# Seven block products for the output of a SwiGLU feed-forward, with weight sums made in DRAM

## The chip, the cores and the metric

The kernel runs on one core of a Trainium2 chip. The metric is the device time of one execution, in microseconds (us). A core has a matrix engine (TensorE, PE in the profile; PEld is its loading of stationary operands), a vector engine (VectorE, DVE), a scalar engine (ScalarE, ACT), a general engine (GpSimd, POOL) and a queue engine (SyncE, SP), which here only issues transfers. POOL issues transfers too, among them all that add to what is in the destination.

## The reference

One decoder layer on 512 tokens of width 1024, in float32: half a SwiGLU feed-forward, a mixer (a state-space scan beside differential attention), cross-attention into 256 memory positions, half of a second SwiGLU feed-forward, and a final norm. The change is in the last but one step:

```
def swiglu(h, w_in, w_out):
    gate, up = jnp.split(h @ w_in, 2, axis=-1)
    return (jax.nn.silu(gate) * up) @ w_out

x = x + 0.5 * swiglu(rms_norm(x, norm_ffn2_w), ffn2_w_in, ffn2_w_out)   # 1024 -> 2 x 2816 -> 1024
return rms_norm(x, norm_final_w)
```

## The kernel before

Activations lie transposed, features on the 128 partitions and the 512 tokens along the row; x is eight such tiles. A float32 matrix product is made of three matmuls in a shorter format. Each operand is split in a high part (ACT copies it to fp32r) and a low part (VectorE subtracts that from the original), and the product is high x high + high x low + low x high. split_into (line 146) issues the two instructions. Weights come from DRAM on SP into six buffers wr of 128x1024, and are split into three buffers wh and wl, so that the split of a weight block waits for the matmuls that used the block three before.

A feed-forward goes through its 22 tiles of hidden features in three parts of 8, 8 and 6 (THIRDS). In each part, quads make the hidden tiles, and then an output product adds them to x.

- quad (line 235) makes two tiles of gate and two of up by a scheme of seven block products in place of eight (Winograd's form of Strassen's). Weights are in four blocks b11, b12, b21, b22, and the products need the sums t = b12 + b11, then t + b22 and again + b21 (lines 252 and 254, on VectorE), and m7 = b12 + b22. The first and the last of these are made while loading: raw_w (line 221) loads one block on SP and adds the other with a transfer that POOL issues. The activations' sums, by halves of the tokens (H = 256), are made once for a feed-forward, in block_sums (line 190).
- ffn_quads (line 380) gates: two products with the norm's row, tanh on ACT, three operations on VectorE, and the split of two hidden tiles g.
- The output product of the first feed-forward, and of the first two parts of the second, is by feature: for each of eight output tiles proj (line 272) adds nf x 3 matmuls of 512 columns, and lines 448 and 449 add it to x. This is eight products where the quads have seven.
- The last part of the second feed-forward is by token (class Close, line 1033), so that the result comes out in rows of tokens. For four blocks of 128 tokens and two halves of the width it adds nf x 3 matmuls, with g as the stationary operand; x is transposed on TensorE (turned); then come the update, the final norm (squares on ACT, a power on POOL) and the writing, block by block.

The order of the work is written by generators in Order (line 51). Dense generators run one after the other, a chain is spawned with a delay in estimated TensorE time and steps in when its time has come. SP's queue keeps the order in which the program is traced; the other engines' queues are ordered by a planner from that order, by what it reckons to be ready. Every engine works through its queue in order and waits at the first instruction that isn't ready. The mixer runs between the feed-forwards. In it POOL issues the loads of the attention bias (line 623) and of r (line 763), computes inverse roots (lines 311 and 697) and some sums; upd_2 (line 1018) ends the cross-attention and prepares the second feed-forward. The layout of the weights in DRAM is made on the host, in layout (line 1114).

Of the kernel before, what the change touches and what calls it, by code (L numbers as in the profile page):

```python
# [17 lines left out]
P = 128  # L18
# [12 lines left out]
NSLOT = 56  # L31
NHALF = 14
# [6 lines left out]
MASKED = 8e30  # L39
LAMBDA_INIT = 0.8 - 0.6 * math.exp(-0.3 * 0)  # L40
# [54 lines left out]
def body(tc, a, dbg=None):  # L95
# [22 lines left out]
    def s4(s):  # L118
        return sp.tile([P, 2, 2, T // 2], F32, tag=s, name=nm(s), bufs=1)
# [66 lines left out]

    def hl(pair, sl):
        return pair[0][:, sl], pair[1][:, sl]

    def block_sums(k0, gain, raw):  # L190
# [4 lines left out]
        s12, s34 = s2("s12"), s2("s34")  # L195
        V.tensor_tensor(s12[:, :H], fe[:, H:], fo[:, H:], ALU.subtract)
        V.tensor_tensor(s34[:, :H], fe[:, :H], fe[:, H:], ALU.subtract)
        V.tensor_tensor(s12[:, H:], s12[:, :H], fe[:, :H], ALU.subtract)
        V.tensor_tensor(s34[:, H:], s12[:, H:], fo[:, :H], ALU.add)
        s12, s34 = split("s12", s12), split("s34", s34)  # L200
        lo, hi = slice(0, H), slice(H, T)
        return {
            "11": hl(raw[k0], lo), "12": hl(raw[k0 + 1], lo), "22": hl(raw[k0 + 1], hi),
            S1: hl(s12, lo), S2: hl(s12, hi), S3: hl(s34, lo), S4: hl(s34, hi),
        }
# [29 lines left out]
    def quad(xs, src):  # L235
# [7 lines left out]
        m1, t, m3, m2, m7 = raw_w(b11), raw_w(b12, b11), raw_w(b22), raw_w(b21), raw_w(b12, b22)  # L243
# [8 lines left out]
        V.tensor_tensor(t, t, m3, ALU.add)  # L252
        yield from add_product(b_ps, split_w(t), xs, S2, False)
        V.tensor_tensor(t, t, m2, ALU.add)
# [3 lines left out]
        yield from add_product(a_ps, split_w(m2), xs, "12", False)  # L258
# [4 lines left out]
        yield from add_product(b_ps, split_w(t), xs, "22", False)  # L263
# [113 lines left out]
    def halves(t):  # L377
        return t.rearrange("p (f t) -> p f t", f=2)

    def ffn_quads(xs, wq, st, nq, g, ahead=None):  # L380
        for q_ in range(nq):
            made = None
            for made in quad(xs, next(wq)):
                if made is None:
                    yield
            gs, us = made
            if q_ == nq - 1 and ahead is not None:
                ahead()
            gate, th = s4("gate"), s4("th")
            for i in range(2):  # L390
                row = st.row[:, None, i * H : (i + 1) * H].to_broadcast([P, 2, H])
                V.tensor_tensor(gate[:, i], halves(gs[i]), row, ALU.mult)
            S.activation(th, gate, AF.Tanh, scale=0.5)
            V.scalar_tensor_tensor(gate, th, 1.0, gate, ALU.add, ALU.mult)
            for i in range(2):
                V.tensor_tensor(th[:, :, i], halves(us[i]), gate[:, i], ALU.mult)
            for f in range(2):
                g.append(split("g", th[:, f].rearrange("p a b -> p (a b)")))
            yield
# [11 lines left out]
    def ffn(h, xs, st, wq, wo, on_final=None, first=None, plain=None, close=None, at_out=None):  # L411
        row4 = None
        wq = iter(wq)
        for ti, (f0, nf) in enumerate(THIRDS):
            g = []
            at_end = ti == len(THIRDS) - 1
            if at_end and close is not None:
                close.begin()
            nq = nf // 2
            if ti == 0 and first is not None:  # L420
                for made in ffn_first(h, first):
                    if made is None:
                        yield
                    else:
                        g.append(split("g", gated(*made, st.row)))
                for n in range(NPLAIN - 2):
# [3 lines left out]
                    g.append(split("g", gated(pg, pu, st.row)))  # L430
                    for k0 in range(2 * n, 2 * n + 2, 2):
                        xs.append(block_sums(k0, C_FFN1, h))
# [752 lines left out]
```

## Time and profile before

| | |
|---|---|
| time, median of 3 runs | 1340.49 us (1339.56 to 1343.92) |
| time of the profiled execution | 1342.28 us |
| its span, first to last instruction | 1340.4 us |
| TensorE, VectorE, ACT, POOL busy | 99%, 71%, 47%, 8% of the span |
| granted TensorE clock | 0.997 |
| second feed-forward, first quad to last matmul | some 1000 to 1333 us |
| transfers | 167.89 MB, mean 125 GB/s |

A row of a group has the line, engine and operation, what it writes and reads with shapes, how often, the busy time with the mean ns of one, and the idle time before it with what ended it. A matmul's own duration is longer than its distance to the next, since they overlap; the distance is read from the chain of waits, whose rows are the start, the length, the engine, the tile, the line and the count. Rows of a queue have the start, the length and, in brackets, the idle time before and what ended it. "Landing" is the time from a transfer's issue to its last byte.

### The profile page before, as it was taken

To read this page: it belongs to the slowest core of one execution; us is meant where nothing else is said; L and a number is where in the kernel's file an instruction comes from. 1 tells how busy PE (TensorE), PEld (TensorE's weight loads), DVE (VectorE), ACT (ScalarE), POOL (GpSimd) and SP (SyncE) were. 2 spreads that over 40 slices of the span, in tenths; PEclk is the share of its full clock that TensorE was granted. 3 is DMA by queue.
4 is the path that set the end of the run, shared out by engine and by line. 5 is a ranking of instruction groups with operands and counts; after the bars stand their busy time and mean duration, and the time that the engine had idled before them with its cause. 6 is when DMAs were issued, how large, how long until landed. Compare 5 with 4: busy or idle time off the path is not lost.

```text
span 1340.4 us, 19873 instructions
## 1 busy us (share of the span) xinstructions
PE 1321.4 (99%) x7831; PEld 1149.7 (86%) x7831; DVE 951.1 (71%) x1480; ACT 631.5 (47%) x1070; POOL 104.0 (8%) x123
## 2 busy tenths in 40 slices
PE   8999999999999999999999999999999999999997
PEld 7888999899897778877888887888889989998996
DVE  6775688477886586557877777556788747875774
ACT  6442455144554465346654656334455424542453
POOL 1000001010020001100011031000011000000000
PEclk9999999999999999999999999999999999999999
DMA  7434577466352214421173574321347645745641
GB/s 269 110 111 127 127 205 236 114 139 192 126 168 64 87 36 91 146 91 56 48 140 78 96 140 152 105 70 64 89 117 178 180 129 124 195 139 126 174 111 63
DMA packets 52156, 167.89 MB, mean 125 GB/s; under 512 B 6632, under 2 KB 9168, under 8 KB 52064
## 3 DMA queue, kind: packets, MB, share of 16 engines
q1 hardware_dynamic: 43056, 136.67, 32.1%
q0 software_dynamic: 9008, 29.97, 13.7%
q8 instruction: 61, 1.00, 0.3%
q14 instruction: 31, 0.25, 0.1%
HBM read 164.45 MB, written 4.77 MB: 126 GB/s over the span
## 4 chain that ended last, share of the span: by engine, by line
PE 91%; DVE 3%; DMA 1%; ACT 1%; issue 1%; POOL 1%; POOLq 0%; ACTq 0%; DVEq 0%
PE po L140 17%; PE qb L218 12%; PE qe L218 8%; PE pm L140 8%; PE qa L218 8%; PE pxbc L140 7%; PE pk L140 3%; PE pq L140 3%; PE pcq L140 3%; PE pv L140 3%; PE pz L140 3%; PE pf L140 2%; PE pg L140 2%; PE pu L140 2%; PE ps L140 2%; DMA r<-cum_d 1%
## 5 line engine op out<-in xcount | busy, mean ns | idle before, releaser
L149 ACT ACTIVATE wh<-wr 128x1024 fp32r<-128x1024 f32 (+2 forms) x285 | 292.5, 1028 | 386.1 <-PE po L140 117.4
L150 DVE TENSOR_TENSOR wl<-wr,wh 128x1024 fp32r<-128x1024 f32 (+2 forms) x285 | 337.8, 1186 | 105.6 <-ACT wh L149 103.3
L140 PE MATMUL po<-gh,wh 128*128 128x512 f32 x304 | 118.6, 392 | 0.0
L140 PE MATMUL po<-gl,wh 128*128 128x512 f32 x304 | 118.1, 390 | 0.0
L140 PE MATMUL po<-gh,wl 128*128 128x512 f32 x304 | 117.9, 389 | 0.0
L218 PE MATMUL qa<-hmh,wl 128*128 128x256 f32 x304 | 86.2, 284 | 0.0
L218 PE MATMUL qa<-hml,wh 128*128 128x256 f32 x304 | 86.0, 283 | 0.0
L218 PE MATMUL qa<-hmh,wh 128*128 128x256 f32 x304 | 86.0, 283 | 0.0
L448 DVE TENSOR_TENSOR upd<-po,row 128x512 f32<-128x512 f32 x40 | 27.6, 691 | 74.2 <-PE po L140 74.0
L140 PEld LDWEIGHTS po<-gh,wh 128*128 128x128 f32 x304 | 56.9, 188 | 13.6 <-ACT gh L149 2.1
L140 PEld LDWEIGHTS po<-gl,wh 128*128 128x128 f32 x304 | 57.1, 188 | 12.6 <-DVE gl L150 1.0
L140 PEld LDWEIGHTS po<-gh,wl 128*128 128x128 f32 x304 | 57.1, 188 | 11.6
L218 PEld LDWEIGHTS qa<-hmh,wl 128*128 128x128 f32 x304 | 58.3, 192 | 0.4 <-DVE wl L150 0.4
L218 PEld LDWEIGHTS qa<-hmh,wh 128*128 128x128 f32 x304 | 58.3, 192 | 0.2
L218 PEld LDWEIGHTS qa<-hml,wh 128*128 128x128 f32 x304 | 58.3, 192 | 0.2
L140 PE MATMUL pxbc<-hnh,wh 128*128 128x512 f32 x128 | 52.3, 408 | 0.0
L140 PE MATMUL pxbc<-hnl,wh 128*128 128x512 f32 x128 | 50.2, 392 | 0.0
L140 PE MATMUL pxbc<-hnh,wl 128*128 128x512 f32 x128 | 50.2, 392 | 0.0
L639 ACT ACTIVATE ec<-ec,mn 128x512 f32<-128x512 f32 (+3 forms) x64 | 35.4, 555 | 25.0 <-DVE mn L638 25.0
L226 POOL DMA_DIRECT2D wr<-in_f2q x22 | 19.0, 863 | 362.0 <-DVE wl L150 114.2
L218 PE MATMUL qe<-s12h,wh 128*128 128x256 f32 x152 | 44.0, 290 | 2.7 <-ACT wh L149 1.7
L218 PE MATMUL qe<-s12h,wl 128*128 128x256 f32 x152 | 43.8, 288 | 0.8 <-DVE wl L150 0.8
(375 smaller groups left out, 3779.8 us busy)
## 6 DMA issues: line engine op xcount, KB each, us to landing
wr<-in_f2q SPq DMA_DIRECT2D x55, 512.0 KB, 4.0
wr<-in_f1q SPq DMA_DIRECT2D x40, 512.0 KB, 4.3
wr<-in_f2q POOLq DMA_DIRECT2D x22, 512.0 KB, 6.9
wr<-in_f2o SPq DMA_DIRECT2D x22, 512.0 KB, 4.2
wr<-in_f1q POOLq DMA_DIRECT2D x16, 512.0 KB, 6.4
wr<-in_f1o SPq DMA_DIRECT2D x16, 512.0 KB, 4.7
wr<-in_wxbc SPq DMA_DIRECT2D x16, 512.0 KB, 3.5
wr<-in_f1i SPq DMA_DIRECT2D x8, 512.0 KB, 6.9
```

Source lines behind the costliest of these rows:

```text
L140: nc.tensor.matmul(out, w, x, start=start, stop=stop)
L149: S.activation(hi, src, AF.Copy),
L150: V.tensor_tensor(lo, src, hi.bitcast(F32), ALU.subtract),
L218: nc.tensor.matmul(out, a_[:, wc], b_, start=first and f == 0 and kp == 0 and j == 0, stop=kp == n - 1 and j == 2, skip_group_check=True)
L226: last_sum[:] = [G.dma_start(raw, m, accum_op=ALU.add).ins]
L448: V.tensor_tensor(upd, po, row4, ALU.mult)
L639: S.activation(ec[:, :n], ec[:, :n], AF.Exp, bias=mn, scale=-1.0, accum_out=sm[c][:, i : i + 1])
```

## The change

The output product of the second feed-forward is now by token in all three parts, and made by the same scheme of seven products as the quads. The blocks are: hidden tiles in pairs (even, odd), tokens in halves of 256, the width in halves of 512. g is the stationary operand, in blocks of 128 tokens, and the weights stream in 512 columns. Each product keeps its sums for two blocks of tokens in two PSUM banks.

What comes with it:

- The hidden tiles are kept as blocks and as sums of blocks (block_tiles, sums_of), made right after gating, on ACT and VectorE, once for each quad.
- Four sums of the output weights' blocks are made in DRAM (out_sums): for each part and sum, one copy from DRAM to DRAM on SP, and two transfers that add on POOL. The chain is spawned 60 us (estimated) after the end of the first feed-forward.
- In the quads of the second feed-forward (by_transfer), t + b22 is no longer made on VectorE. b22 is loaded a second time into a buffer t2, and a transfer on POOL adds t to it. The next sum, t4, is made on VectorE after m2 has been split, in m2's buffer.
- x is transposed right after the cross-attention (turn, 22 us after its last update), in place.
- Updates and the final norm are by block of tokens; in the last part the last product takes its blocks one after the other (by_pair).
- The slots for 128x512 tiles go from 56 to 55, those for 128x256 from 14 to 16. ffn is now ffn1 for the first feed-forward, whose work is the same, and ffn2. The host lays the weights out in blocks.

The diff, cut to its core:

```diff
-NSLOT = 56
-NHALF = 14
+NSLOT = 55
+NHALF = 16
+    def sums_of(b11, b21, b22, b12, pair=None):
+        s31, s24 = s2("s31"), s2("s24")
+        if pair is None:
+            V.tensor_tensor(s31[:, :H], b11, b21, ALU.subtract)
+            V.tensor_tensor(s31[:, H:], b21, b22, ALU.subtract)
+        else:
+            V.tensor_tensor(halves(s31), *pair, ALU.subtract)
+        V.tensor_tensor(s24[:, :H], s31[:, H:], b11, ALU.subtract)
+        V.tensor_tensor(s24[:, H:], s24[:, :H], b12, ALU.add)
+        s31, s24 = split("s31", s31), split("s24", s24)
+        lo, hi = slice(0, H), slice(H, T)
+        return {S3: hl(s31, lo), S1: hl(s31, hi), S2: hl(s24, lo), S4: hl(s24, hi)}
...
-        m1, t, m3, m2, m7 = raw_w(b11), raw_w(b12, b11), raw_w(b22), raw_w(b21), raw_w(b12, b22)
+        m1, t = raw_w(b11), raw_w(b12, b11)
+        if by_transfer:
+            t2, m2, m7, m3 = raw_w(b22, t), raw_w(b21), raw_w(b12, b22), raw_w(b22)
+            t4 = m2
...
-        V.tensor_tensor(t, t, m3, ALU.add)
-        yield from add_product(b_ps, split_w(t), xs, S2, False)
-        V.tensor_tensor(t, t, m2, ALU.add)
+        if not by_transfer:
+            V.tensor_tensor(t2, t, m3, ALU.add)
+        yield from add_product(b_ps, split_w(t2), xs, S2, False)
...
+        w2 = split_w(m2)
+        if by_transfer:
+            V.tensor_tensor(t4, t2, m2, ALU.add)
+        yield from add_product(a_ps, w2, xs, "12", False)
...
+    def block_tiles(g):
+        def made(th):
+            raw = split("g", th[:, 2:4].rearrange("p a b -> p (a b)"))
+            b11 = [s2("g11" + p_, R32, (P, H)) for p_ in "hl"]
+            split_into(*b11, th[:, 0])
+            lo, hi = slice(0, H), slice(H, T)
+            g.append({"11": tuple(b11), "22": hl(raw, lo), "12": hl(raw, hi)} | sums_of(*(th[:, i] for i in range(4)), pair=(th[:, 0:2], th[:, 1:3])))
+        return made
...
+            od.spawn(out_sums(), 60.0)
...
+    def out_sums():
+        for t, (to, of) in enumerate(((B12, B11), (B12, B22), (B22, 0), (B21, 2))):
+            for c in range(len(THIRDS)):
+                blocks = a[f"f2b{c}"]
+                nc.sync.dma_start(wsum[c][t], blocks[to])
+                yield 5.0
+                more = wsum[c][of] if t > 1 else blocks[of]
+                for k in range(0, more.shape[1], D):
+                    ks = slice(k, min(k + D, more.shape[1]))
+                    G.dma_start(wsum[c][t][:, ks], more[:, ks], accum_op=ALU.add)
+                    yield 3.0
+
+    def out_blocks(c, g, col4, last):
+        blocks = a[f"f2b{c}"]
+        n = len(g)
+        parts = [(k, min(k + 2, n)) for k in range(0, n, 2)]
...
+        def some(ps, w, which, part, t, first):
+            ts = slice(t * P, (t + 1) * P)
+            for k in range(*part):
+                (wh, wl), (gh, gl) = w, g[k][which]
+                ws = slice((k - part[0]) * T, (k - part[0] + 1) * T)
+                for j, (a_, b_) in enumerate(((gh, wh), (gl, wh), (gh, wl))):
+                    nc.tensor.matmul(ps, a_[:, ts], b_[:, ws], start=first and k == 0 and j == 0, stop=k == n - 1 and j == 2, skip_group_check=True)
+                yield
...
+        both = [product(a_ps, blocks[B11], "11", True), product(e_ps, sums[0], S1, True)]
+        for _ in parts:
+            for m in both:
+                for _ in range(2 * 2):
+                    if next(m, 1) is None:
+                        yield
...
+        for t in range(2):
+            S.activation(b_ps[t], a_ps[t], AF.Copy)
...
+        yield from product(b_ps, sums[2], S2)
+        for t in range(2):
+            u2.append(s2("u2"))
+            S.activation(u2[t], b_ps[t], AF.Copy)
+            V.tensor_tensor(e_ps[t], e_ps[t], u2[t], ALU.subtract)
+        yield from product(a_ps, blocks[B21], "12")
+        for t in range(2):
+            update(t, 0, a_ps[t])
+        yield from product(b_ps, sums[1], S3)
+        for t in range(2):
+            c22 = s2("c22")
+            V.tensor_tensor(c22, p5[t], b_ps[t], ALU.subtract)
+            update(t + 2, 1, c22)
+        yield from product(e_ps, blocks[B22], S4)
+        for t in range(2):
+            update(t, 1, e_ps[t])
+            if last is not None:
+                last(t)
+        for t, m in enumerate([product(b_ps, sums[3], "22", by_pair=last is not None)]):
+            yield from m
+        for t in range(2):
+            update(t + 2, 0, b_ps[t])
+            if last is not None:
+                last(t + 2)
```

More of the change, by code (lines that the diff above doesn't have):

```diff
@@ L375, in gated, with ffn_quads @@
         return gate
[L377 to L384, printed above, removed]
+    def ffn_quads(xs, wq, st, nq, made, places, by_transfer=False):
+        for _ in range(nq):
+            for out in quad(xs, next(wq), by_transfer):
+                if out is None:
                     yield
-            gs, us = made
-            if q_ == nq - 1 and ahead is not None:
-                ahead()
+            gs, us = out
             gate, th = s4("gate"), s4("th")
@@ L1098, in body @@
+    od.add(ffn2())
     od.run()
```

236 lines of the change are left out of this document (128 added, 108 removed).

## The prediction

> **What bounds the kernel now.** I read the page first, then the busy time by stretches, then the chain of waits, then the groups by shape, and last the queues of VectorE and of the transfers inside one quad.
>
> ```profile
> span 1340.4 us, 19873 instructions
> PE 1321.4 (99%) x7831; PEld 1149.7 (86%) x7831; DVE 951.1 (71%) x1480; ACT 631.5 (47%) x1070; POOL 104.0 (8%) x123
> ```
>
> TensorE is busy 99% of the span. What it no longer has to do is gained, as long as the other queues deliver in time. The stretches of the second feed-forward show how much room those have; the columns are the stretch, its length, then PE, PEld, DVE, ACT, POOL, clock, DMA share and GB/s. The second row is one quad (seven products over 256 columns), the third one output product; the first lies in the mixer.
>
> ```profile
> 425.00:560.00 135.00, 135.00 (x706) 108.63 (x705) 90.16 (x192) 72.16 (x172) 10.87 (x13) 1.00 0.33 89
> 1027.16:1047.32 20.16, 20.16 (x171) 20.16 (x170) 16.85 (x19) 10.75 (x13) 1.70 (x2) 1.00 0.75 182
> 1067.48:1111.41 43.93, 43.92 (x195) 35.89 (x194) 24.50 (x29) 10.66 (x12) 2.56 (x3) 1.00 0.49 129
> ```
>
> TensorE has no gap in any of them, at full clock. In a quad VectorE is busy 16.85 of 20.16 us; in the output product 24.50 of 43.93. The chain of waits gives the price of a matmul:
>
> ```profile
> 1053.09 2.88 PE qb L218 x24
> 1058.84 2.88 PE qb L218 x24
> 1064.60 2.88 PE qb L218 x24
> 1067.48 5.47 PE po L140 x24
> 1072.96 38.45 PE po L140 x168
> 1301.89 1.64 PE pxf L144 x15
> ```
>
> A matmul of 512 columns costs 38.45 / 168 = 0.2289 us, one of 256 columns 2.88 / 24 = 0.12 us, a transpose 0.11 us. The output product starts on the heels of the last quad (1064.60 + 2.88 = 1067.48), so even the gating of the last quad is covered now.
>
> **The change on TensorE.** The groups by shape give the counts of the two old output stages, by feature (po) and by token (pf), one of three equal rows of each, then the transposes and their copies:
>
> ```profile
> L140 PE MATMUL po<-gh,wh 128*128 128x512 f32 x128 | 49.8, 391 | 0.0
> L140 PE MATMUL pf<-wfh,gh 128*128 128x512 f32 x48 | 18.9, 401 | 0.0
> L144 PE MATMUL pxf<-ident,x 128*128 128x128 f32 x32 | 4.5, 272 | 0.0
> L1050 ACT ACTIVATE xt<-pxf 128x512 f32<-128x512 f32 x8 | 4.5, 592 | 6.3 <-PE pxf L144 6.3
> ```
>
> That is 3 x (128 + 48) = 528 matmuls of 512 columns. The new stage has seven products, each of (4, 4, 3) tile pairs x 2 token blocks x 3 parts: 168 + 168 + 126 = 462, and one matmul with ones. 65 fewer x 0.2289 = **-14.9 us**. The 32 transposes stay; they move from the end into the first quads (turn), with eight ACT copies of 0.59 us, where ACT is busy 10.75 of 20.16: nothing gained or lost.
>
> **The change on VectorE and ACT.** Prices:
>
> ```profile
> L150 DVE TENSOR_TENSOR wl<-wr,wh 128x1024 fp32r<-128x1024 f32 x98 | 119.8, 1223 | 31.8 <-ACT wh L149 31.3
> L150 DVE TENSOR_TENSOR gl<-th,gh 128x512 fp32r<-128x512 f32 x22 | 14.9, 687 | 2.3 <-ACT gh L149 2.3
> L196 DVE TENSOR_TENSOR s<-fe,fo 128x256 f32<-128x256 f32 x4 | 1.7, 424 | 0.1
> L1082 DVE SCALAR_TENSOR_TENSOR xt<-pf,col,xt 128x512 f32<-128x512 f32 x8 | 6.0, 750 | 7.1 <-PE pf L140 7.1
> L149 ACT ACTIVATE wh<-wr 128x1024 fp32r<-128x1024 f32 x98 | 103.7, 1059 | 152.1 <-PE po L140 60.8 <-PE qb L218 22.9 <-DVE wr L252 21.1
> L251 ACT ACTIVATE p<-qe 128x512 f32<-128x512 f32 x11 | 6.4, 579 | 0.0
> ```
>
> In an output stage of four pairs, 14 weight splits cost VectorE 14 x 1.22 = 17.1 us; eight updates of 0.75, two c22 and two subtractions of 0.69 make 8.8. That is 25.9 of 168 x 0.2289 = 38.5 us. ACT has 14 x 1.06 + 6 x 0.58 = 18.3. Each split (1.06 + 1.22) feeds 12 matmuls, 2.75 us, and three buffers look two parts ahead: covered, 0. Without that cover each part would wait up to 2.3 us.
>
> The quads are the tighter place. One of the two adds of weight blocks (t + m3, 1.22) goes to a transfer; two gl (1.37) become a raw gl 0.69, a g11 0.42, s31 0.69, two s24 of 0.42, and two lows of 0.69: 4.02. VectorE rises by 4.02 - 1.37 - 1.22 = 1.4 to about 18.3 of 20.16 us. The load is not even; this is its crowded stretch, the gating of the quad before among the splits of the next:
>
> ```profile
> 1046.71 1.23 DVE L252 TENSOR_TENSOR wr<-wr,wr 128x1024 f32<-128x1024 f32 x1
> 1053.76 1.22 DVE L150 TENSOR_TENSOR wl<-wr,wh 128x1024 fp32r<-128x1024 f32 x1
> 1055.56 1.23 DVE L150 TENSOR_TENSOR wl<-wr,wh 128x1024 fp32r<-128x1024 f32 x1
> ```
>
> The fifth product (m7) starts at 1058.84 and its low half is there at 1056.8: a margin of 2.1 us. The t4 add moves behind m2's split but stays ahead of m7's low half, and the add that leaves stood ahead of the stretch. So up to 4.02 - 1.37 = 2.65 us more may come before it: 0.5 us late, some 1.0 if the lows wait for ACT too. From below it is 0, if the queue takes the weights first. I take 0.4, nearer the margin's 0.5, for the 8 quads that have a gated quad before them: **+3.2** (0 to 8).
>
> **The transfers in a quad.** Before: five loads and two accumulating transfers (b11 onto t, b22 onto m7). After: six loads and three; the new one adds t onto t2 and needs t's own to have landed. The two queues' shares are of a stretch of 290 us (1000 to 1290); then the issues, with the median time to landing, the extremes of POOL's, what SP waits for, and one POOL issue:
>
> ```profile
> q1 hardware_dynamic: 9535, 34.73, 38.2%
> q0 software_dynamic: 2736, 9.96, 20.8%
> wr<-in_f2q SPq DMA_DIRECT2D x46, 512.0 KB, 4.2
> wr<-in_f2q POOLq DMA_DIRECT2D x19, 512.0 KB, 7.4
> ...
> DMA to landing us min/median/max: 5.3/7.4/8.0
> ...
> SPq L224 <- DVE wl L150: 196.5, 46, 13.0
> ...
> 1044.23 0.85 POOL L226 DMA_DIRECT2D wr<-in_f2q  x1 [13.34 <-DMA wr<-in_f2o]
> ```
>
> A load takes 0.382 x 290 / 34.73 x 0.524 = 1.67 us of all 16 engines, an accumulating one 0.208 x 290 / 9.96 x 0.524 = 3.17. A quad goes from 5 x 1.67 + 2 x 3.17 = 14.7 us (0.73 of it, as the stretch shows) to 19.5, 0.97. The six buffers now hold exactly one quad, and SP waits for one to be split free. t2's load can start about when m7 is split, 9.5 us after the quad's start; it lands 4.2 later, POOL issues (0.85), the addition lands 7.4 later: 21.95. Split (1.06 + 1.22): 24.2. Product t2 of the next quad starts at 20.16 + 2 x 2.88 = 25.9. Margin 1.7 us, so 0 from below. From above, landings that grow as the share does (x 0.97 / 0.73) take 3.8 us more: 2.1 late. I take 0.3, since the margin holds at today's landings, for 10 quads: **+3.0** (0 to 21). POOL stands still for t's landing; behind it waits only m7's transfer, which has two products more to land.
> The Trainium skill, page "DMA: Bandwidth & Descriptors", section "Bandwidth", puts the limit at about 358 GB/s of HBM for a core; eight of the nine transfers read HBM, an estimated 208 GB/s by that, so this term would be 0 and the sum 3.0 lower. The stretch's DMA share of 0.75 at 182 GB/s speaks against so much room.
>
> **Edges of the stages.** The gating of a third's last quad reaches its splits here:
>
> ```profile
> 1072.27 1.15 ACT L149 ACTIVATE gh<-th 128x512 fp32r<-128x512 f32 x2 [2.86 <-DVE th L396]
> ```
>
> That is 4.8 us after the quad's end at 1067.48. Its new "11" block is split second, about 1.7 us on (two ACT halves of about 0.5, a low of 0.69): 6.5 us after the quad. The interleaved first parts of two products cover 24 matmuls, 5.5 us, and one more pair 0.7 in the thirds of four: 0.3 + 0.3 + 1.0 = **+1.6** (0 to 4).
>
> **The tail.** Now the last of four token blocks ends like this:
>
> ```profile
> 1332.76 0.75 DVE L1082 SCALAR_TENSOR_TENSOR xt<-pf,col,xt 128x512 f32<-128x512 f32 x1
> 1335.33 0.54 POOL L1091 TENSOR_TENSOR frr<-fv,mhalf 128x1 f32<-128x1 f32 x1 [3.06 <-DVE fv L1089]
> 1337.07 0.38 SPq L1095 DMA_DIRECT2D out<-xt  x1
> ```
>
> The blocks are a matmul chain (18 x 0.2289 = 4.1 us) apart. After the change two blocks end together, 4.1 us before TensorE does, and the last two 2.06 us apart. The last update may queue behind another block's final multiplication, which waits for POOL: **+1.0** (0, if they interleave; 6, if four chains of 3.7 run one after the other).
>
> **The mixer.** It gets 12 copies in DRAM on SP and 24 accumulating transfers on POOL, each behind its copy: 24 x 0.85 = 20.4 us of POOL where it is busy 10.87 of 135, and where the DMA share is 0.33. Queued behind a waiting POOL are rr, ncol, bias and the r loads:
>
> ```profile
> r<-cum_d POOLq DMA_DIRECT2D x4, 256.0 KB, 12.0
> ...
> 514.56 3.04 POOL L763 DMA_DIRECT2D r<-cum_d  x4
> ...
> 530.36 0.61 ACT L821 ACTIVATE e<-r 64x512 f32<-64x512 f32 x1
> ...
> 539.80 1.02 PE py L140 x16
> ```
>
> The first r lands at 514.56 + 0.75 + 12 = 527.3 and is used at 530.4, 3 us later: the cover. A transfer in front (7.4) would exceed it by 4. I take **+0.5** (0 to 4). One slot fewer (55) and the altered block sums do the same work: 0. The sums themselves are needed after 1067: ready long before.
>
> **Sum.** -14.9 + 3.2 + 3.0 + 1.6 + 1.0 + 0.5 = **-5.6 us**. The profiled execution's own time, 1342.28, becomes 1336.7. It stands 1.8 above the median 1340.49, so the median becomes **1334.9**.
>
> **Rivals.**
> (B) All cover holds; only the tail and a little at the edges is paid: -14.9 + 1.4 = -13.5, 1327. For: TensorE shows no gap in a quad with VectorE at 84%. Against: 18.3 of 20.16 and a margin of 2.1.
> (C) VectorE and transfers together eat the gain: 1.0 in each of 11 quads, 1.6 + 1.0 at edges and tail: -14.9 + 13.6 = -1.3, 1339. For: both late arrivals fall into the same stretch of the quad. Against: they overlap rather than add.
> (D) Slower: the transfer onto t2 becomes the bound. The quad then lasts as long as buffer, load, two landings, split and m7's split. From landings of 4.2 + 7.4 = 11.6 it stalls above 13.3, and from about 14.5 the gain is gone ((14.9 - 3.1) / 10 = 1.2 a quad). At the upper end, 2.1 x 10 + 3.1 - 14.9 = +9, 1349.5. For: 0.97 of the engines. Against: the longest of POOL's landings in the old quads is 8.0.
> The Trainium skill, same page, section "Issuing engines are not separate DMA queues", says that transfers from POOL and SP interleave on the same 16 engines; by that rule D's price holds in full. The trace agrees: the two queues' prices add up to 0.73 of a quad, and the quad's row shows 0.75.
> (E) The mixer decides: POOL, waiting for copies, holds up the r loads of a group and one set of rr and ncol by 4 us each beyond their cover: 8 in place of 0.5, +1.9 in all, 1342.4. For: POOL takes its queue in order. Against: the DMA share of 0.33 there. That the products save no matmuls can't be, since the loops fix their number.
>
> **Chances.** Forecast (-2 to -11, 1329.5 to 1338.5) 0.45; B 0.22; C 0.15; D 0.14; E 0.04. A measurement of this kernel can tell about 0.3%, 4 us. Faster by more: 0.38 of the forecast and all of B, 0.60. Within: 0.07 of the forecast, 0.12 of C, 0.02 of E, 0.21. Slower: D and the rest, 0.19. The range takes in B and the nearer part of D: 1326 to 1346.
>
> **What would show it.** Right: output stages of 38.5, 38.5 and 28.8 us without gaps; waits of TensorE in the quads for wl (VectorE's term) or for wh behind a transfer (t2's term), adding up to 6 us; quads of 20.4 to 21 us. B: quads still 20.16. D: POOL's transfers landing after 9 us and quads over 21.4. E: gaps between 425 and 700 that were not there. I am wrong if the output stages themselves show gaps.

## The result, and the profile after

The changed kernel takes 1382.4 us (median of five runs, 1377.3 to 1384.4), the kernel before 1339.6 (five runs, 1338.4 to 1343.9): a ratio of 1.031, 95% interval 1.028 to 1.034. It is slower, by far more than rival D allowed; 1334.9 was forecast. The profiled execution took 1377.29 us.

The head of the profile page of the changed kernel, its span and its busy times:

```profile
span 1375.3 us, 20006 instructions
PE 1319.3 (96%) x7766; PEld 1145.8 (83%) x7766; DVE 978.0 (71%) x1533; ACT 667.3 (49%) x1124; POOL 135.0 (10%) x158
```

TensorE's 65 matmuls are gone (7831 to 7766), and yet its busy time falls by only 2 us, mostly because part of its work ran on a slower clock; and it stood still for 37 us more. The times from the first matmul of a stage to the first of the next add up to the span, so they say where the 34.9 us between the two profiled executions came from. The medians differ by 42.8, and the profiled execution of the changed kernel was its fastest of five, so some of the loss of the others isn't in this table (to about 0.1 us):

| us | before | after | difference |
|---|---|---|---|
| up to the first quad of the second feed-forward | 983.3 | 989.1 | +5.8 |
| quads, first third (with the moved transposes) | 84.0 | 89.2 | +5.2 |
| output stage, first third | 43.9 | 38.3 | -5.6 |
| quads, second third | 80.7 | 89.2 | +8.5 |
| output stage, second third | 43.9 | 38.4 | -5.5 |
| quads, last third, up to the last stage's first matmul | 60.5 | 76.1 | +15.6 |
| last stage and tail | 44.1 | 55.0 | +10.9 |

Busy times by stretch of the changed kernel (stretch, length, PE, PEld, DVE, ACT, POOL, clock, DMA share, GB/s): first output stage, second third's quads, second output stage, and then the end piece by piece.

```profile
1078.25:1116.60 38.35, 38.35 (x170) 31.38 (x169) 30.32 (x36) 20.85 (x25) 2.57 (x3) 1.00 0.71 205
1116.60:1205.75 89.15, 83.23 (x673) 82.34 (x673) 65.99 (x79) 44.00 (x55) 7.75 (x9) 0.98 0.78 207
1205.75:1244.20 38.45, 38.45 (x170) 31.42 (x169) 30.36 (x36) 20.86 (x25) 2.58 (x3) 1.00 0.68 206
1311.04:1320.35 9.31, 0.28 (x4) 0.08 (x2) 7.03 (x12) 4.36 (x7) 0.00 (x0) 0.75 0.00 0
1320.35:1325.00 4.65, 4.61 (x10) 3.21 (x11) 2.94 (x3) 1.41 (x2) 0.00 (x0) 0.50 0.43 129
1347.52:1359.93 12.41, 0.39 (x3) 0.01 (x1) 4.42 (x12) 4.50 (x10) 1.50 (x2) 0.73 0.45 148
```

The first two output stages do what the sum said: 38.35 and 38.45 us without a gap. The second third's quads have 6 us of idle TensorE in 89, and the last stage has two holes, 9.31 us ahead of it and 12.41 in it. Behind the first, ten matmuls take 4.65 us in place of 10 x 0.2289 = 2.3, at a clock of 0.50.

What TensorE waited for, over the whole execution (total, times, longest):

```profile
PE ob L1115 <- ACT wh L151: 12.0, 1, 12.0
PE oa L1115 <- ACT wh L151: 9.0, 1, 9.0
PE qb L231 <- ACT u L277: 8.4, 8, 2.6
PE py L142 <- DVE r L852: 5.1, 2, 3.8
PE qb L231 <- ACT qb L267: 3.5, 4, 1.7
```

Four places, then. In the quads the wait is for the copies u and qb out of PSUM, not for wl or for a transfer's wh, where I had looked. The chain of waits through the hole in the last stage:

```profile
1352.72 0.73 ACT x L1194
1353.46 0.33 SPq L1195
...
1353.89 0.39 SPq L1197
...
1354.34 4.37 DMA wr<-wsum
...
1358.82 1.06 ACT wh L151
...
1359.93 1.22 PE ob L1115 x2
```

SP takes its queue in order. The writes of the finished token blocks (L1195, L1197) wait for the norm's last multiplication (L1194), and the loads for the last product stand behind them. ACT at the start of the last stage:

```profile
1312.14 1.06 ACT L412 ACTIVATE th<-gate 128x1024 f32<-128x1024 f32 x1 [8.83 <-DVE gate L411]
1318.72 0.63 ACT L151 ACTIVATE s24h<-s 128x512 fp32r<-128x512 f32 x1 [0.29 <-DVE s L204]
1319.26 1.99 ACT L151 ACTIVATE wh<-wr 128x1024 fp32r<-128x1024 f32 x2
```

The splits of the first output weights come last, behind the whole gating of the last quad, though ACT had been idle for 8.83 us before it. In the mixer, POOL:

```profile
523.18 1.72 POOL L1089 DMA_DIRECT2D wsum<-wsum  x2 [7.53 <-DMA wsum<-in_f2b]
524.30 2.94 POOL L790 DMA_DIRECT2D r<-cum_d  x3
```

POOL stood 7.5 us at a sum whose copy hadn't landed, and the r loads behind it were issued 10 us later than before (514.56). In the quads, ACT:

```profile
1184.97 1.06 ACT L151 ACTIVATE wh<-wr 128x1024 fp32r<-128x1024 f32 x1 [4.01 <-DMA wr<-wr]
1185.93 1.04 ACT L412 ACTIVATE th<-gate 128x1024 f32<-128x1024 f32 x1
1187.83 0.58 ACT L267 ACTIVATE qb<-qa 128x512 f32<-128x512 f32 x1
1195.40 0.63 ACT L151 ACTIVATE s24h<-s 128x512 fp32r<-128x512 f32 x1 [1.36 <-DVE s L204]
1196.41 0.59 ACT L277 ACTIVATE u<-qb 128x512 f32<-128x512 f32 x1
```

The split of t2 waits 4 us for the new transfer, with tanh and the copy qb behind it; the sums' halves, waiting for VectorE, stand ahead of u.

### The profile page after: what moved, and what is told of

Same layout as the page of the kernel before. It is cut to its first block, busy times and chain, and to the rows that moved or that the text cites. A ratio compares the mean times of both kernels' runs of the same rounds, so it can differ in the third digit from the quotient of the medians.

```text
span 1375.3 us, 20006 instructions
## 1 busy us (share of the span) xinstructions
PE 1319.3 (96%) x7766; PEld 1145.8 (83%) x7766; DVE 978.0 (71%) x1533; ACT 667.3 (49%) x1124; POOL 135.0 (10%) x158
## 5 line engine op out<-in xcount | busy, mean ns | idle before, releaser
L142 PE MATMUL po<-gh,wh 128*128 128x512 f32 x176 | 68.8, 392 | 0.0
L142 PE MATMUL po<-gl,wh 128*128 128x512 f32 x176 | 68.5, 390 | 0.0
L142 PE MATMUL po<-gh,wl 128*128 128x512 f32 x176 | 68.4, 389 | 0.0
L231 PE MATMUL qb<-s31h,wh 128*128 128x256 f32 x152 | 44.4, 292 | 8.4 <-ACT u L277 8.4
L231 PE MATMUL qb<-s24h,wh 128*128 128x256 f32 x152 | 44.4, 292 | 3.6 <-ACT qb L267 3.5
L231 PE MATMUL qe<-s31h,wh 128*128 128x256 f32 x152 | 44.0, 290 | 1.7 <-ACT wh L151 1.7
L231 PE MATMUL qe<-s31h,wl 128*128 128x256 f32 x152 | 43.8, 288 | 0.8 <-DVE wl L152 0.8
L231 PE MATMUL qe<-s31l,wh 128*128 128x256 f32 x152 | 43.9, 288 | 0.2 <-DVE s31l L152 0.2
L231 PE MATMUL qb<-s24l,wh 128*128 128x256 f32 x152 | 43.7, 288 | 0.0
L231 PE MATMUL qb<-s24h,wl 128*128 128x256 f32 x152 | 43.7, 287 | 0.0
L474 DVE TENSOR_TENSOR upd<-po,row 128x512 f32<-128x512 f32 x24 | 16.6, 690 | 38.1 <-PE po L142 38.0
```

The lines of the kernel that those rows point to most:

```text
L142: nc.tensor.matmul(out, w, x, start=start, stop=stop)
L231: nc.tensor.matmul(out, a_[:, wc], b_, start=first and f == 0 and kp == 0 and j == 0, stop=kp == n - 1 and j == 2, skip_group_check=True)
L474: V.tensor_tensor(upd, po, row4, ALU.mult)
```

## The experiments

Ratios are to the kernel before, timed in the same batch, with 95% intervals; stage times are from one profiled execution each.

### Four causes, one at a time

**e1: the last product's loads ahead of the output writes.**

```diff
         yield from product(e_ps, blocks[B22], S4)
+        raws = [load(sums[3], part) for part in parts] if last is not None else []
...
-                ws = [weights(of, part) for part in parts]
+                ws = [weights(of, part, raw) for part, raw in zip(parts, raws)]
```

> The two weight loads of the very last product are issued on SP before the output writes of the first two token blocks; nothing else moves. Theory (order in a queue): the 12.4 us gap of TensorE in the last stage is the loads waiting behind writes that wait for the norm, and the 9 matmuls at half clock after it cost another 2; both go, so some 13 us less than the changed kernel, about 1369 us. Rival (transfers are simply late there): a gap of at least 4.2 us landing and 2.3 us split remains, 6 us less.

Measured: 1369.3 us, ratio 1.022 (1.020 to 1.024). The last stage and tail take 43.0 us in place of 55.0: the hole is gone, and SP's rows show the loads ahead now:

```profile
1335.37 1.83 SPq L1101 DMA_DIRECT2D wr<-wsum  x2
1354.35 0.34 SPq L1200 DMA_DIRECT2D out<-x  x1
```

The cause of the 12.4 us is SP's order.

**e2: the gain loads behind the last stage's fourth product** (the one with "12", called the third in the expectations, where the first two, interleaved, count as one), where SP had issued them ahead of the stage's weights.

```diff
         for t in range(2):
             update(t, 0, a_ps[t])
+        if last is not None:
+            gains()
...
-            if at_end:
-                for n in range(2):
-                    gain.append(s2("gain"))
-                    nc.sync.dma_start(gain[n], a["final"][n].partition_broadcast(P))
```

> The two small loads of the final norm's gain are issued after the fourth product of an output stage instead of ahead of the last stage; nothing else moves. Theory (the planner placed the splits of the last stage's first weights behind the gating because it reckoned the loads behind the gain loads to be late): the 9.3 us gap at the start of the last stage falls under 1 us and the slow clock after it goes: some 10 us less, about 1372 us. Rival (ACT and VectorE are full there): the gap stays over 5 us, at most 4 us less.

Measured: 1374.9 us, ratio 1.026 (1.022 to 1.030). The hole at the start of the last stage is gone: its first matmul follows the last quad's within 0.1 us, at full clock, because ACT's splits stand ahead of tanh again:

```profile
1323.13 1.06 ACT L151 ACTIVATE wh<-wr 128x1024 fp32r<-128x1024 f32 x1 [1.77 <-PE qe L231]
1326.01 0.63 ACT L151 ACTIVATE wh<-wr 128x512 fp32r<-128x512 f32 x1 [1.82 <-PE qb L231]
1326.85 1.06 ACT L412 ACTIVATE th<-gate 128x1024 f32<-128x1024 f32 x1 [0.21 <-DVE gate L411]
```

Two small loads decided where the planner put three splits. In this execution r kept TensorE waiting for 12.4 us in the mixer, which is why the span doesn't show the gain.

**e3: both adds on VectorE again** in these quads (no transfer onto t2).

```diff
-            yield from ffn_quads(xs_2, wq, st_2, nf // 2, block_tiles(g), BY_BLOCK, True)
+            yield from ffn_quads(xs_2, wq, st_2, nf // 2, block_tiles(g), BY_BLOCK, False)
```

> In the second feed-forward's quads the sum t + b22 is made on VectorE again (as before), with five loads and two adding transfers a quad; all else as in the changed kernel. Theory (the transfer onto t2 lands late and blocks ACT's queue): quads of 20.2 to 20.7 us, the three stretches of quads some 12 us shorter in all, about 1370 us. Rival (VectorE, at 18.3 of 20.16 us, is the bound in the quads): with 1.2 us more a quad they stay at 22 us or get longer, 1382 us or more.

Measured: 1387.7 us, ratio 1.035 (1.033 to 1.037): slower still. The quads take 94, 92 and 76 us to the next stage (89, 89 and 76 with the transfer), and in the second third ACT's splits now wait for VectorE's add:

```profile
ACT wh L151 <- DVE wr L272: 11.1, 4, 3.2
```

So the transfer alone is not the cause. Whichever engine makes t2, its split is late in ACT's queue.

**e4: no sums in DRAM**, plain blocks read in their place.

```diff
-            od.spawn(out_sums(), 60.0)
...
-        sums = wsum[c]
+        sums = [blocks[B12], blocks[B12], blocks[B22], blocks[B21]]
```

> Leaves out the copies and sums in DRAM: the four products that need sums read plain blocks of weights instead, so the output is that of other weights; loads and matmuls are as many. Theory (the sums' transfers hold up the loads of r in the mixer): the second feed-forward starts 5 us earlier, at 984 instead of 989 us, and the rest is the same: about 1377 us. Rival (the 5 us are not the sums'): 1382 us, start at 989.

Measured: 1373.3 us, ratio 1.023 (1.019 to 1.027). The second feed-forward starts at 982.4 us, as before the change (983.3), and TensorE waits 1.6 us for r in place of 5.1. The quads stay at 90, 88 and 78 us: the mixer's loss comes from the sums, the quads' loss doesn't. The executions with the sums in this place spread: the second feed-forward starts at 991.2 in e1, 998.8 in e2 and 990.5 in e3, and at 989.1 in the changed kernel, with the same code in the mixer.

### The queues put right, then the quads

**e5: three edits together**: those of e1 and e2, and the sums begun 403 us (estimated) later.

```diff
-            od.spawn(out_sums(), 60.0)
+            od.spawn(out_sums(), 463.0)
```

> Three edits at once, none in a quad: the four loads of the last product's sums are issued ahead of the output writes, the two gain loads stand behind the third product of the last stage, and the sums in DRAM are begun about 400 us later, behind the mixer's r loads and in cross attention, where POOL had nothing to do. Theory (the loss has four places: SP's queue at the end, ACT's queue at the start of the last stage, POOL's queue in the mixer, and the quads): the gaps of 12.4 and 9.3 us, the 4.8 us of the mixer and some 3 us of slow clock behind the gaps go, so 34.9 - 29 = about 6 us of loss stay in all with the saving of 14.9 already in them: 1346 to 1352 us, with the quads as in the changed kernel (89, 89 and 67 us to the next stage). Rival (the transfers of the sums cost wherever they lie): the wait for r goes but the first quads or the projections of cross attention get as much longer, and the time stays above 1353.

Measured: 1361.2 us, ratio 1.015 (1.011 to 1.019), over the expected range. The last stage and tail take 43.0 us and the quads 89, 91 and 64, as the theory says; but the second feed-forward starts at 994.9, with new waits for r and for the norm's diagonal of 4 us and more. The rival was right on the sums: their cost went with them.

**e6: t2 summed in DRAM**, on top of e5. In this kernel and in e8, the very last quad also makes t2 on VectorE and takes t4's weights for its fourth product, so its output differs.

```diff
-            t2, m2, m7, m3 = raw_w(b22, t), raw_w(b21), raw_w(b12, b22), raw_w(b22)
+            t2, m2, m7, m3 = raw_w(by_transfer.pop(0)), raw_w(b21), raw_w(b12, b22), raw_w(b22)
...
+            nc.sync.dma_start(qsum[q], b22)
+            yield 8.0
+            for more in (b12, b11):
+                G.dma_start(qsum[q], more, accum_op=ALU.add)
+                yield 8.0
```

> As the kernel with the three queue edits, and t2 of the eleven quads is summed in DRAM during the mixer as the output's sums were (a copy and two accumulating transfers each, 8 us apart), so that a quad loads it and has no transfer onto t2. VectorE and ACT do the same work as in the changed kernel. Theory that t2's transfer is late and holds ACT's queue: the quads of the second and third stretch fall from 89 and 67 us to about 82 and 62, and the time is 10 to 14 us under the kernel with the three edits alone. Theory that VectorE and ACT have too much to do before the copies: no more than 4 us under it, and TensorE still waits for the copies u and qb in every gated quad.

Measured: 1363.7 us, ratio 1.017 (1.014 to 1.020). The quads fall to 89, 83 and 63 us, 10 less in all than in e5 (245 to 235). But the eleven sums more put the start of the second feed-forward at 1002.6, with 12 us of waits for mn, which VectorE makes from the attention's scores and their bias, in the mixer.

**e7: the sums s31 and s24 of a gated quad deferred**, on top of e5, to behind the next quad's fifth product.

```diff
         yield from add_product(b_ps, split_w(m7), xs, S3, False)
+        while later:
+            later.pop()()
```

> As the kernel with the three queue edits, and the sums s31 and s24 of a gated quad are made behind the next quad's fifth product (m7) and not among its first splits; the last quad of a third makes them at once. Transfers are as in the changed kernel. Theory that ACT's queue is crowded by the sums' copies ahead of p and u: the waits for u (8.4 us, up to 2.6 each) fall under 3 and the time is 6 to 9 us under the kernel with the three edits alone. Theory that the late transfer onto t2 alone holds ACT: the waits move to other lines and the time is within 3 us of it.

Measured: 1348.1 us (ten runs, 1342 to 1355), ratio 1.006 (1.003 to 1.008). The waits for u are all but gone (0.5 us) and the quads take 90, 84 and 63 us, 7.3 less than in e5, inside the expected 6 to 9. The rest of the 13 us between the medians isn't from the quads: with the same code in the mixer, this profiled execution reached the second feed-forward at 985.9 and the other at 994.9. So a single profile fixes the mixer's cost no closer than some 9 us.

**e8: e6 and e7 together.**

> t2 summed in DRAM and the sums of the gated quad deferred, on top of the three queue edits. If each takes its own part, TensorE has no gap over 0.3 us in a gated quad: the stretches of quads are those of before plus the transposes (84, 81 and 61 us with 3.5 in the first), the output stages 38.4, 38.4 and 29, and the time about 1342.3 - 14.9 + 3 = 1330 us, 1328 to 1335. If one cause stands behind both, it is no faster than the better of the two.

Measured: 1358.5 us, ratio 1.013 (1.012 to 1.015). The quads take 87.9, 80.6 and 60.9 us: those of before plus 3.9, 0 and 0.4, the first with 3.5 us of transposes. So these two causes account for the quads' loss; the time that was to come out (1328 to 1335) is lost in the mixer (start at 1006.7).

### Cheaper repairs

**e9: squares and gains of half rows early, copies two steps ahead of their adds**, on top of e7.

```diff
             update(t + 2, 1, c22)
+        if last is not None:
+            for t in range(2):
+                last(t, 0)
+                last(t + 2, 1)
...
+            if i + 2 < len(jobs):
+                copy(i + 2)
+                yield 4.0
```

> The kernel with the three queue edits and the deferred sums, and two more edits: the squares and the multiplication by the gain are done for each half row of the output as soon as it is complete, and the copies of the sums in DRAM are issued two steps ahead of their accumulating transfers, some 20 us earlier. Theory of the tail (the chains of two token blocks stand behind each other on VectorE and ACT, and 12.1 us pass from the last matmul's start to the end of the span): it falls to 8 to 9 us. Theory of the mixer (POOL stands still at a sum whose copy hasn't landed, and the norm's column behind it waits): the wait of TensorE for ndiag (4.5 us) goes. Together 6 to 8 us under the kernel with the deferred sums: 1338 to 1343. Rivals: the earlier work of the tail delays splits in the last stage; the landing of the transfers and not the wait for the copies is what costs, and the wait for ndiag stays.

Measured: 1358.3 us, ratio 1.012 (1.008 to 1.015): worse than e7. Both theories fell. The tail is shorter, but the last stage has a wait of 2.2 us in its place (43.1 us together, 43.0 in e7), and the norm's column now waits longer, not less:

```profile
PE nrow L142 <- DVE ndiag L348: 16.1, 2, 15.6
PE qb L231 <- ACT qb L267: 6.8, 8, 1.5
PE ob L1147 <- DVE wl L152: 3.5, 3, 2.2
```

**e10: seven raw buffers**, on top of e9.

```diff
-NSLOT = 55
+NSLOT = 53
...
-        raw = wp.tile([P, D], F32, tag="wr", name=nm("wr"), bufs=6)
+        raw = wp.tile([P, D], F32, tag="wr", name=nm("wr"), bufs=7)
```

> As e9_tail_and_copies with seven raw weight buffers in place of six (and two slots fewer), so that each load, and t2's with it, starts one split of weights (about 2.9 us) earlier. Theory that the transfer onto t2 lands late because its load waits for a buffer: TensorE's waits for the copy qb (6.0 us) fall to 2 or less and the time is 4 to 6 us under e9. Rival (the landings are long because the queues share 16 engines at a share of 0.8): the transfers land as much later and the time is within 2 us.

Measured: 1363.8 us, ratio 1.016 (1.013 to 1.018). In the quads the theory holds: the wait for qb falls from 6.8 to 1.0 us, and they take 88.0, 80.6 and 60.5. The whole is 5 us slower than e9, since TensorE waits 14.3 us for r, at 763 us above all. Whether the two slots that it gave up are the cause wasn't tried.

**e11: the copy qb ahead of t2's split**, on top of e9.

```diff
+        with behind([copied] if by_transfer else []):
+            w_t2 = split_w(t2)
```

> As e9_tail_and_copies, with the split of t2 in the second feed-forward issued behind the copy of qa into qb, so that tanh and this copy no longer stand behind a split that waits for the transfer. Theory that the order of ACT's queue, not the landing itself, makes TensorE wait: waits for qb and u go, waits for wl or wh of t2 take at most 2 us in their place, and the time is 3 to 6 us under e9. Rival: TensorE waits for t2 itself as long as it did for the copy; within 1.5 us.

Measured: 1354.1 us, ratio 1.008 (1.005 to 1.011), 4.2 us under e9. Nothing was done to the transfer, and yet the quads take 87.8, 81.8 and 61.6 us, with 0.5 us idle in the second third:

```profile
1125.10:1206.85 81.75, 81.25 (x673) 80.78 (x672) 65.68 (x79) 44.20 (x55) 7.86 (x9) 1.00 0.81 220
```

The transfers onto t2 landed after a median of 7.6 us, in e9 after 6.9. So with t2 as late as before, it was the order in ACT's queue that made TensorE wait; e10 shows that a t2 loaded earlier takes the wait for qb away as well. What is left is in the same profile, on POOL:

```profile
884.68 0.81 POOL L1112 DMA_DIRECT2D wsum<-wsum  x1 [3.82 <-DMA wsum<-in_f2b]
885.22 1.33 POOL L339 TENSOR_TENSOR ncol<-nv,mhalf 128x4 f32<-128x4 f32 x1
```

The column's operand nv was ready at 869.84; POOL came to it 15 us later, behind three sums that waited for copies. The copies landed late (a median of 14.8 to 16.6 us, 8.3 to 8.6 in the changed kernel's mixer), and the 16 engines were full, which is the likely reason. The stretch ahead of it, in e11 and then in the kernel before, has DMA shares of 1.03 and 0.33:

```profile
840.00:872.00 32.00, 32.00 (x146) 26.34 (x144) 17.38 (x24) 11.52 (x16) 4.93 (x6) 1.00 1.03 300
```

```profile
840.00:872.00 32.00, 32.00 (x146) 26.47 (x145) 18.96 (x25) 12.74 (x18) 0.27 (x1) 1.00 0.33 103
```

**e12: e10 and e11 together.**

> Seven buffers and the copy before t2's split, on e9_tail_and_copies. If no cause but the named ones is left, the stretches of quads are as before plus 3.5 us of transposes in the first (87.5, 81, 61), the output stages 38.4, 38.4 and 30, the tail 8.5, the mixer as before: 1340.4 - 14.9 + 1.5 = 1327 us of span, 1328 to 1333 with what lies around it, faster than the kernel before by 0.5 to 1%. If it is not under 1338, something is still unnamed.

Measured: 1364.8 us, ratio 1.017 (1.014 to 1.019). Quads of 87.7, 80.7 and 60.6 us and output stages of 38.4, as expected; but r and the norm's column cost 11 and 16 us, and the second feed-forward starts at 1013.9. The sum was right for the stages and wrong for the mixer.

### The sums around the r loads

**e13: a pause.** The sums start where the changed kernel starts them, and the last quarter waits until POOL has issued the first r loads. Late gain loads, deferral and the copy's place stay, the copies two steps ahead don't; the last product is split ahead of the output's scaling.

```diff
         for t, (to, of) in enumerate(((B12, B11), (B12, B22), (B22, 0), (B21, 2))):
+            if t == 3:
+                yield 55.0
```

> The kernel with the late gain loads, the deferred sums and the copy ahead of t2's split; the sums in DRAM are begun where the changed kernel begins them, but the last quarter of them waits 55 us more, so that POOL issues the four r loads of the first group ahead of it and not behind a copy that hasn't landed; the last product's weights are loaded and split ahead of the output's scaling, and the squares and gains of complete half rows are done at once. Theory (what is left of the loss is POOL's queue standing at a copy, with the r loads or the norm's column behind it): the second feed-forward starts at 983 to 986 us as before, its quads and products take 308 us to the last stage as with the copy ahead, the last stage 41: a span of 1332 to 1336, a time of 1334 to 1338, faster by 0.2 to 0.5%. Rival (copies and adding transfers cost by their bytes wherever they stand): the second feed-forward starts after 988 and the time is 1340 or more.

Measured: 1338.9 us (twelve runs, 1334.9 to 1342.9), ratio 0.998 (0.9965 to 0.9992). The second feed-forward starts at 985.9, with no wait for r in the list. POOL issues the first r loads ahead of the last quarter of the sums:

```profile
519.56 3.11 POOL L802 DMA_DIRECT2D r<-cum_d  x4
570.48 1.79 POOL L1103 DMA_DIRECT2D wsum<-wsum  x2
```

**e14: the sums spread over a longer time**, as e13 without the pause.

```diff
-                yield 5.0
+                yield 20.0
...
-                    yield 3.0
+                    yield 8.0
```

> As e13_sums_around_r without the pause, and with each copy 20 us ahead of its adding transfers and these 8 us apart, so that the sums take about 430 us in place of 170. If only a wait of POOL for copies costs, this is as good as e13 (within 3 us), since hardly any copy is late. If transfers on the same 16 engines make r and weights land late, TensorE waits for r or weights in several places of the mixer, 5 us or more in all, and it is slower than e13.

Measured: 1359.9 us, ratio 1.014 (1.012 to 1.017), start at 1004.6, and 10.2 us of waits for r in four places. It doesn't tell POOL's order from the transfers' load, as it was meant to: some copies landed too late even so, and the first r loads stood behind such a sum again:

```profile
530.53 1.80 POOL L1101 DMA_DIRECT2D wsum<-in_f2b  x2 [7.80 <-DMA wsum<-in_f2b]
531.72 3.69 POOL L802 DMA_DIRECT2D r<-cum_d  x4
```

**e15: e13 with the tail as in the changed kernel.**

> As e13_sums_around_r with the tail of the changed kernel's form: the squares and gains of a token block at its end, and the last product's weights loaded early but split where they are used. Theory that two chains of token blocks behind each other make the tail 12 us in place of 8: 2 to 4 us slower than e13. Rival (the tail's earlier work only moves the delay into the last products): within 1 us of e13.

Measured: 1337.5 us (twelve runs, 1333.0 to 1341.9), ratio 0.9973 (0.996 to 0.999): no slower than e13. The work moved forward in the tail gains nothing (43.1 us against 43.0). This is the fastest version found, and it beats the kernel before by 0.3% (0.1 to 0.4). Its stretches: the three groups of quads, then the last stage with the tail.

```profile
986.70:1075.20 88.50, 87.04 (x717) 85.84 (x717) 71.98 (x93) 51.14 (x68) 10.16 (x11) 1.00 0.71 188
1113.60:1196.70 83.10, 81.68 (x674) 80.89 (x673) 65.66 (x79) 44.16 (x55) 7.74 (x9) 1.00 0.79 217
1235.10:1296.20 61.10, 60.83 (x505) 60.56 (x504) 48.00 (x57) 32.56 (x40) 5.16 (x6) 1.00 0.78 203
1296.20:1339.30 43.10, 29.92 (x128) 23.14 (x126) 32.15 (x55) 23.61 (x43) 2.97 (x4) 0.91 0.40 132
```

Against the stages of before these differ by +4.5, +2.4, +0.6 and -1.0 us, the output stages by -5.5 each, and the start by +3.4.

## Why the prediction was wrong, step by step

**The saving on TensorE (-14.9)** was right. The first two output stages came out at 38.35 and 38.45 us for the 38.5 forecast. The sentence that named gaps in the output stages as the sign of an error held for the third one.

**The tail (+1.0, 0 to 6)** is the first step that failed. Its question was how four chains share VectorE, ACT and POOL. It didn't ask which queue the output writes stand in: SP's, ahead of the last product's loads, 12.4 us. The prediction listed neither in SP's order. Beside that, the chains took 12.1 us from the last matmul's start to the end in e5 and e7, 8.1 before: +4.0, within the bounds. Two attempts did not shorten stage and tail together.

**The edges (+1.6, 0 to 4)** are the second. The working followed the new block "11" down its queue and took for granted that weight splits stand ahead of it, as they did in the old kernel. In the first two thirds they do, and nothing was lost there; in the last, two gain loads turned the order round: 9.3 us, and about 2.3 for the slow clock behind it.

**VectorE's crowded stretch (+3.2) and the transfer onto t2 (+3.0)** are the third. The two operands were late, as it said, but the size was wrong and so was the place where TensorE feels it: the quads lost 20.0 us up to the last matmul of the last one (5.2 + 8.5 + 15.6 - 9.3), of which 3.5 are the transposes. The working followed the late operand to the one product that uses it, with a margin of 1.7 us, and named waits for wl or wh as the sign. The copies out of PSUM that share ACT's queue were counted as busy time only. Once a split waits for a transfer, or a sum's half for VectorE, the next copy waits too, and with it a product whose weights are ready. Taken away from the 245 us of quads in e5, the gated sums among the splits are worth 7.3 us (e7) and the transfer onto t2 is worth 10 (e6), 15.2 together (e8), where the sum had 3.2 and 3.0. The copy's place alone took 5.8 (237.0 in e9 to 231.2 in e11). D's mechanism, a landing that sets the quad's length, wasn't it: in the changed kernel t2's transfers landed after a median of 6.5 us, less than the 7.4 assumed, and e11 lands t2 no earlier than e9.

**The mixer (+0.5, 0 to 4)** is the fourth. Rival E described what happened, POOL waiting for copies ahead of the r loads, at 4 of 100. Measured was a start of the second feed-forward 5.8 us later, near E's 8, and 7 to 16 later in e1 to e3, with the same code there. The error in method was to weigh E against the forecast as if one excluded the other: E could come on top, and did. E's argument against itself, a DMA share of 0.33, was the share without the sums: no working added their bytes to it. The stretch that it was read from has 0.72 in the changed kernel, and the r loads in it land after a median of 17.1 us in place of 12.0:

```profile
425.00:560.00 135.00, 129.91 (x672) 104.24 (x671) 86.50 (x190) 68.58 (x169) 21.47 (x26) 0.97 0.72 181
```

**The slow clock** was in no term. In the changed kernel TensorE worked for 24 us at a granted clock of 0.50, in the kernel before for 6.5. Half of that is lost, so it cost some 9 us more, which are spread over the stages above.

With these repairs (e15) the time is 1337.5 us, 2.9 under the kernel before on the same chip, where the sum had -5.6. In the profiled execution the span is 1.1 under, 4.5 short of the sum. The last stage with the tail is where most of it stands: 44.1 us less 4.1 for 18 matmuls and 3.5 for the transposes, and 2.0 more for edge and tail, would be 38.5, and it takes 43.1; the tail alone has 4.0 in place of 1.0. The start has 3.4 in place of 0.5. The quads, 4.0 longer without the transposes, are by now within the 6.2 of their two terms.

What stays open: how much of the mixer's loss in the changed kernel is POOL's order and how much the load of the sums' transfers on the same engines (e14 did not part them); why seven buffers make r late; what would shorten the tail.

## What to carry to other kernels

For each instruction that a change adds or lets wait, list what stands behind it in its own engine's queue, not only who uses its result; an engine busy half of the time can still hold up TensorE by its order. Do that for SP and POOL too, at both ends of the kernel: loads behind output writes, and loads behind a transfer that waits for another. Causes that can come together aren't rivals, and their prices add up or nearly so (7.3 and 10 us alone, 15.2 together in the quads).

## What the hardware showed unexpectedly

After the 9.31 us gap the granted clock was 0.50 for 4.65 us, and matmuls of 512 columns started 0.43 us apart in place of 0.229. The Trainium skill, page "TensorE: Matmul & The Clock Gate", section "What's actually happening", has half rate after an idle window of about 3.4 us, in windows that run freely; the trace agrees for the long gaps.

Shorter gaps did both. The longest wait for u in the second third was 2.6 us in the changed kernel and in e5. Behind it the changed kernel ran at full clock, e5 at half, and the place of the gap on a fixed grid in time tells them apart. In the 17 traces here, every stretch of half clock that ends within the span lasts a multiple of 3.41 us (3.41 to 17.07), and within a trace all of them begin whole multiples of 3.41 us apart. Each of the next two views shows two neighbouring windows of that grid, first in the changed kernel, then in e5:

```profile
1192.75:1196.17 3.42, 1.72 (x15) 1.51 (x13) 3.42 (x6) 2.06 (x4) 0.00 (x0) 1.00 0.39 113
1196.17:1199.58 3.41, 2.53 (x21) 2.53 (x22) 3.41 (x5) 1.77 (x3) 0.00 (x0) 1.00 0.84 293
```

```profile
1199.78:1203.19 3.41, 1.29 (x11) 1.08 (x10) 3.41 (x6) 2.05 (x4) 0.00 (x0) 1.00 0.54 145
1203.19:1206.60 3.41, 2.96 (x14) 2.96 (x15) 3.41 (x5) 1.34 (x2) 0.00 (x0) 0.50 0.84 298
```

In the changed kernel the boundary cut the gap in two, and TensorE was idle for 1.70 us of the first window; in e5 it was idle for 2.1, and the next window ran at half clock. Over all windows for which the traces have the clock, none at full clock with less than 1.67 us of idle TensorE was followed by half clock, and none with more than 1.91 us by full clock. So here it was enough that TensorE was idle for about half of a window, where the Trainium skill's page has an idle window. In e5 that cost half of the 2.96 us of work in the next window, 1.5 us; in the changed kernel the same gap cost nothing of the kind.

The sums' adding transfers with a plain source (512 KB) landed after a median of 10.7 us in the changed kernel's mixer and of 14.7 in e11's cross attention, where the loads of the same size took medians from 4.1 to 17.6. The price of 7.4 us that the prediction used was that of quads. So an adding transfer has no one price.
